# One queue of expert weights: issuing loads in reading order and varying the small expert's lag

## The chip, the cores and the metric

The kernel runs on 1 core of a Trainium2 chip. The metric is the device time of one execution in microseconds. The kernel before takes 1853.82 us (median of 3 runs, 1853.0 to 1855.28).

## What is computed

Two transformer-like blocks of two layers each on 256 tokens of width 1024. The change touches the last stage only, the mixture of experts of the second block: each token goes to the 2 best of 8 experts.

```python
logits = x @ router_w
top_v, top_i = lax.top_k(logits, TOP_K)              # TOP_K = 2 of N_EXPERTS = 8
gates = jax.nn.softmax(top_v, axis=-1)
combine = sum(one_hot(top_i, 8) * gates[..., None], axis=-2)
for e in range(8):                                   # D_FF_EXPERT = 3584
    y = y + combine[..., e:e+1] * ((silu(x @ w_gate[e]) * (x @ w_up[e])) @ w_down[e])
x = layer_norm(DEEPNORM_ALPHA * x + y, ln_ffn_g, ln_ffn_b)
```

The three weight matrices of the 8 experts are 336 pieces of 1 MB (128 partitions x 2048 floats). Each is read once from memory.

## The kernel before

**Blocks.** The experts are put in 8 places. The even places 0, 2, 4, 6 are "many" places with 128 token slots, the odd places 1, 3, 5, 7 are "few" places with 64 slots (32 in place 7), and the experts with fewer tokens go to the odd places. Each place is cut into 7 blocks (e, b) of 512 hidden columns. A block needs 6 pieces of weights: two of gate (`mgate`), two of up (`mup`), two of down (`mdown`).

**A many block** splits each piece: ScalarE rounds it to a high part (L437, into one of three `whi` buffers) and VectorE subtracts that for a low part (L438). TensorE multiplies the tokens' high and low parts with the high piece and the high part with the low piece: 8 + 4 matmuls for a piece. **A few block** uses the pieces as they are (`passing`), in plain fp32 matmuls that sit side by side in the array: gate and up of one half (hf) are read together, by `proj_few`.

**The order of blocks** is one list for everything. `at` gives many block i the place i in it and few block i the place i + `BEHIND`; the list is sorted by this. With `BEHIND` at 2.5 all along, three many blocks come first, then few and many alternate, and two few blocks are left at the end.

**Inside the loop over blocks** (L2021) block n projects its gate and up pieces, and between them `turn` transposes the hidden values of block n - 1; then `down` of block n - 1 follows. So for a few block n after a many block, TensorE reads: gate and up of half 0, gate and up of half 1, then the two down pieces of block n - 1. All these matmuls are chained in the order in which the program lists them (`self.line`, `kept`).

**The loads.** Every piece is one DMA of 1 MB on SyncE's queue (L385). `self.order` chains them in the order of the calls. A load goes to the next place in `self.ring`, a first-in first-out list of some 17 places of 1 MB (`raw`, `room`, `xlo`, `x`, and for the first 36 turns `my` and `oht`). It can be issued only once TensorE has read what was there, and the loads behind it wait too. A piece that is split keeps one place: its low part goes into the place left over from the piece before (`low`). For a few block after a many block the calls come in this order: the two down pieces of block n - 1 (L2044, kept in `WD`), gate and up of half 0, gate and up of half 1 (L1903). The loads of an expert other than that of place 0 use its number from a register, which SyncE reads (L2024) ahead of that expert's first load.

Of the kernel before, what the change touches and what calls it, by code (L numbers as in the profile page):

```python
# [33 lines left out]
RANKS = (None, 3, 0, 4, 1, 5, 2, 6)  # L34
SLOTS = (128, 64, 128, 64, 128, 64, 128, 32)

BEHIND = 2.5, 2.5

SPLITS = (("dsa_q", 256), ("dsa_k", 64), ("dsa_v", 64), ("idx_q", 256), ("idx_k", 32), ("idx_w", 8),
          ("fox_q", 384), ("fox_k", 384), ("fox_v", 384), ("fox_f", 6), ("nsa_q", 384), ("nsa_kc", 128),  # L40
# [243 lines left out]
class Net:  # L284
# [1410 lines left out]
    def _moe(self, x, out):  # L1695
# [9 lines left out]
        at = self.psum("t")  # L1705
        hold, kept = self.hold, []
        for tb in range(2):
            ts = slice(tb * 128, tb * 128 + 128)
            with self.ahead(5000):
# [22 lines left out]
                b = nc.vector.tensor_scalar(oh[:, tb, 0], self.c["iota"], slot[:, tb, 0:1], None, op0=ALU.is_equal)  # L1732

                for c in range(2):
# [5 lines left out]
                    i = self.split(xh[:, tb, cs], xl[:, tb, cs], p)  # L1740
                    if tb:
                        self.after(i, b)
                        b = i
# [19 lines left out]
        def back(oh, dt):  # L1763

            ohf = oh.bitcast(F32) if dt is F32R else oh
            oht = self.late.tile([128, NE, T], dt, name="oht", tag="oht")
            for e in range(0, NE, 2):
                p = self.psum()
                for i in range(2):
                    for tb in range(2):  # L1770
                        t = self.tr(p[:, i * 256 + tb * 128:i * 256 + tb * 128 + 128], ohf[:, tb, e + i], self.ident)
                        self.after(t, gm)
                i = nc.scalar.copy(oht[:, e:e + 2], p.rearrange("p (e t) -> p e t", e=2))
                self.after(i, gx)
            return oht
# [63 lines left out]
        i = nc.vector.tensor_copy(cnt, p)  # L1839
# [32 lines left out]
        def block_of(n, q, b, hf):  # L1872

            if q == 0:
                return d[n][0, b, hf]
            return d[n][bass.ds(expert[q], 1), b, hf].rearrange("e p n -> (e p) n")

        H, YD, PP, WD = {}, {}, {}, {}

        def proj(e, b, n, steps=iter(())):  # L1880

            es = slice(0, 128)
            p = self.psum()
            for hf in range(2):
                w = block_of(n, e, b, hf)
                h, lo = self.weights(w, hold=early.pop(0), pieces=range(4)) if early else self.weights(w)
                for i in range(4):
                    k, cs = hf * 4 + i, slice(i * 512, i * 512 + 512)
                    self.mm(p, gh[:, k, es], h[:, cs], start=k == 0, stop=False)
                    self.mm(p, gl[:, k, es], h[:, cs], start=False, stop=False)  # L1890
                if hf:
                    next(steps, None)
                for i in range(4):
                    k, cs = hf * 4 + i, slice(i * 512, i * 512 + 512)
                    self.mm(p, gh[:, k, es], lo[:, cs], start=False, stop=k == KC - 1)
                next(steps, None) if hf == 0 else None
            PP[e, b, n] = p

        def proj_few(e, b, hf):

            p = PP[e, b] = PP.pop((e, b)) if hf else self.psum()
            with self.ahead(3000):
                ws = [self.passing(block_of(n, e, b, hf)) for n in ("mgate", "mup")]  # L1903
            m = SLOTS[e]
            n = 8 * m
            for i in range(4):
                k = hf * 4 + i
                for r in range(0, 128, m):
                    w, c = ws[r // 64], r % 64 // m * n
                    self.mm(p[r:r + m, 0:n], FX[e][:, k, 0:m], w[:, i * 512 + c:i * 512 + c + n], start=k == 0,  # L1910
                            stop=k == KC - 1, tile_position=(0, r), skip_group_check=True)

        def act(e, b):
            sg = self.xp.tile([128, 512], F32, name="msg", tag="sq", bufs=2)
            if e % 2:
                n = 8 * SLOTS[e]
                nc.scalar.copy(sg[:, 0:n], PP.pop((e, b))[:, 0:n])
            else:
                self.after(nc.scalar.activation(sg, PP.pop((e, b, "mgate")), AF.Silu), self.parted[0])
                self.after(nc.vector.tensor_tensor(sg, sg, PP.pop((e, b, "mup")), op=ALU.mult), self.parted[1])  # L1920
            H[e, b] = sg

        def turn(e, b):
            sg = H.pop((e, b))
            pt = self.psum("t")
            m = SLOTS[e]
            for i in range(4 if m == 128 else m // 16):
                self.tr(pt[:, i * 128:i * 128 + 128], sg[:, i * 128:i * 128 + 128], self.ident)
            if e % 2:

                n, h = m // 16, 64 // m
                pv = pt[:, 0:n * 128].rearrange("p (i a m) -> p a i m", i=n, a=2)
                fs, fh = (sg[:, j * 256:j * 256 + n * 64].rearrange("p (i m) -> p i m", i=n) for j in range(2))
                nc.scalar.activation(fs, pv[:, 0], AF.Silu)
                nc.vector.tensor_tensor(fh, fs, pv[:, 1], op=ALU.mult)
                H[e, b] = [fh[:, f % n, f // n * m:f // n * m + m] for f in range(4)]
                return
            i = (7 * (e // 2) + b) % 2
            hh, hl = mh[:, i, 0], mh[:, i, 1]
            i = nc.scalar.copy(hh, pt), nc.vector.tensor_tensor(hl, pt, hh.bitcast(F32), op=ALU.subtract)  # L1940
            if (e, b) in WD:

                for a, p in zip(i, self.parted):
                    self.after(a, p)
            H[e, b] = hh, hl
# [67 lines left out]

        mh = None
        many, few = ([(e, b) for e in range(i, NE, 2) for b in range(7)] for i in range(2))
        at = {f: i + np.interp(i, (0, len(few) - 1), BEHIND) for i, f in enumerate(few)}
        at.update((m, i) for i, m in enumerate(many))
        blocks = sorted(at, key=at.get)
        first = blocks.index(few[0])
# [1 line left out]
        for n, (e, b) in enumerate(blocks):  # L2021
            if n == 2:
                for q in range(1, NE):
                    expert[q] = nc.values_load(idi[0:1, q:q + 1], engines=(mybir.EngineType.SP,), min_val=1, max_val=NE - 1)  # L2024
            if n == 9:

                mc = hw.tile([128, 1], F32, name="mc")
                over = hw.tile([128, 8], F32, name="over")

                nc.vector.memset(cap[:, 0:1], 128.0)  # L2030
                nc.vector.tensor_scalar(cap[:, 1:8], rank[:, 1:8], 2.5, 64.0, op0=ALU.is_lt, op1=ALU.mult)
                nc.vector.tensor_scalar(over[:, 1:8], rank[:, 1:8], 5.5, 32.0, op0=ALU.is_lt, op1=ALU.mult)
                nc.vector.tensor_tensor(cap[:, 1:8], cap[:, 1:8], over[:, 1:8], op=ALU.add)
                nc.vector.tensor_scalar(cap[:, 1:8], cap[:, 1:8], 32.0, None, op0=ALU.add)
                nc.vector.tensor_tensor(over, cnt, cap, op=ALU.subtract)
                nc.vector.tensor_reduce(mc, over, axis=AX.X, op=ALU.max)
                nc.vector.tensor_scalar(mc, mc, 0.0, None, op0=ALU.max)
                mci = hw.tile([128, 1], I32, name="mci")
                nc.vector.tensor_copy(mci, mc)
            if n == 7:  # L2040
                oht = back(oh, F32R)
            steps = iter(())
            if e % 2 and blocks[n - 1][0] % 2 == 0:
                WD[blocks[n - 1]] = [self.weights(block_of("mdown", *blocks[n - 1], hf)) for hf in range(2)]  # L2044
            if e % 2:
                proj_few(e, b, 0)
            else:
                proj(e, b, "mgate")
            if n == 1:
                mh = hw.tile([128, 2, 2, 512], F32R, name="mh", tag="mh")  # L2050
            if n:
                turn(*blocks[n - 1])
            if n + 1 == first:
                steps = gather(0, some=False)
            if e % 2:
                proj_few(e, b, 1)
            else:
                if b == 6 and e + 2 < NE:
                    steps = gather(e + 2)
                proj(e, b, "mup", steps)  # L2060
            act(e, b)
            if n < 2:

                i = by_place(qcomb, comb) if n else places(oh, qslot, range(1, NE), True)
                self.hold = self.hold[0], i, None
            if n:
                down(*blocks[n - 1], steps)
            for _ in steps:
                pass
            if n > 2 and blocks[n - 2][1] == 6:  # L2070
                scatter(blocks[n - 2][0])
            if n == len(blocks) - 5:
                gb = self.rows()
# [144 lines left out]
```

## Time and profile before

| | |
|---|---|
| time, median of 3 runs | 1853.82 us |
| the profiled execution | 1856.29 us |
| its span, first to last instruction | 1854.5 us |
| TensorE busy in the span | 1783.7 us (96%) |
| VectorE, ScalarE busy | 1073.1 us (58%), 867.3 us (47%) |
| mean granted TensorE clock | 0.982 |
| data moved | 497.71 MB, mean 268 GB/s |

The expert stage runs from about 1000 us to the end. Of its loads the first ten are issued before 975 us. A busy TensorE here is a TensorE that has a matmul under way; matmuls overlap, so the time of one and the distance between the starts of two are different numbers. The page's strip of DMA rates shows 394 to 421 GB/s from about the middle of that stage's first fifth to the end, and 102 to 338 GB/s before that.

### The profile page before, as it was taken

How to read it: one execution, taken by the hardware profiler on the slowest of the kernel's cores; microseconds unless marked ns; L12 is line 12 of the kernel's file. 1: busy time of each engine (PE TensorE's matmuls, PEld its weight loads, DVE VectorE, ACT ScalarE, POOL GpSimd, SP SyncE). 2: the span in 40 equal slices, each digit the busy share in tenths (PEclk: the TensorE clock that was granted, in tenths of full speed). 3: DMA queues.
4: the chain of work that ended last, by engine and by line, in shares of the span. 5: the costliest groups of instructions: out<-in, count | busy, mean ns of one | idle time of the engine just before them, and what ended most of it. 6: DMA issues, size and time to landing. Idle time of an engine off the chain costs nothing. (4 is left out here: it accounts for less than half of the span.)

```text
span 1854.5 us, 27561 instructions
## 1 busy us (share of the span) xinstructions
PE 1783.7 (96%) x11038; PEld 1351.6 (73%) x11038; DVE 1073.1 (58%) x1586; ACT 867.3 (47%) x1291; POOL 33.3 (2%) x78
## 2 busy tenths in 40 slices
PE   7999999999999999999999999999999999999984
PEld 5777788778896999888977766665656566665652
DVE  3765688757644754466437755565556565565543
ACT  3454375545553544345345545444535444444531
POOL 1000010000000000000010000000000000000000
PEclk9999999999999999989998999999999999999997
DMA  9654443234211555543028799999999999999996
GB/s 386 257 225 167 175 160 125 69 115 171 92 54 63 196 184 172 197 146 117 24 102 338 287 398 394 411 413 420 421 421 421 421 421 421 421 421 420 421 420 250
DMA packets 71175, 497.71 MB, mean 268 GB/s; under 512 B 8226, under 2 KB 9538, under 8 KB 11264
## 3 DMA queue, kind: packets, MB, share of 16 engines
q1 hardware_dynamic: 70752, 495.39, 67.8%
q8 instruction: 89, 1.46, 0.3%
q0 software_dynamic: 288, 0.48, 0.1%
q14 instruction: 46, 0.38, 0.1%
HBM read 493.81 MB, written 1.05 MB: 267 GB/s over the span
## 5 line engine op out<-in xcount | busy, mean ns | idle before, releaser
L438 DVE TENSOR_TENSOR raw<-raw,whi 128x2048 fp32r<-128x2048 f32 (+1 forms) x157 | 279.8, 1800 | 198.9 <-ACT whi L437 198.2
L437 ACT CAST whi<-raw 128x2048 fp32r<-128x2048 f32 (+1 forms) x198 | 306.6, 1570 | 160.7 <-PE mm L459 48.6
L413 PE MATMUL mm<-whi,g 128*128 128x512 f32 x896 | 227.3, 396 | 2.5 <-DVE y L2011 2.5
L413 PEld LDWEIGHTS mm<-whi,g 128*128 128x128 f32 x896 | 166.4, 189 | 38.9 <-issue 4.5
L437 ACT CAST whi<-room 128x2048 fp32r<-128x2048 f32 (+1 forms) x97 | 172.9, 1803 | 31.7 <-PE mm L413 13.5
L458 PE MATMUL mm<-xhi,whi 128*128 128x256 f32 x720 | 182.1, 288 | 0.7 <-ACT whi L437 0.7
L459 PE MATMUL mm<-xlo,whi 128*128 128x256 f32 x720 | 180.4, 286 | 0.0
L413 PE MATMUL mm<-room,fx 128*64 128x512 f32 (+1 forms) x632 | 152.1, 526 | 10.6 <-DMA room<-in_mup_dram 7.2
L458 PEld LDWEIGHTS mm<-xhi,whi 128*128 128x128 f32 x720 | 137.7, 191 | 8.1 <-issue 5.6
L459 PEld LDWEIGHTS mm<-xlo,whi 128*128 128x128 f32 x720 | 137.7, 191 | 1.5 <-issue 1.4
L438 DVE TENSOR_TENSOR room<-room,whi 128x2048 fp32r<-128x2048 f32 x47 | 107.6, 2289 | 31.7 <-ACT whi L437 29.7
L413 PE MATMUL s<-whi,mh 128*128 128x512 f32 x448 | 117.2, 404 | 0.0
L413 PEld LDWEIGHTS s<-whi,mh 128*128 128x128 f32 x448 | 82.6, 189 | 37.9 <-issue 19.9
L463 PE MATMUL mm<-xhi,raw 128*128 128x256 f32 x720 | 104.3, 285 | 0.0
L413 PE MATMUL mm<-raw,fx 128*64 128x512 f32 (+1 forms) x344 | 91.5, 508 | 6.5 <-DMA raw<-in_mup_dram 6.5
L1940 ACT CAST mh<-t 128x512 fp32r<-128x512 f32 x28 | 16.4, 585 | 169.5 <-PE t L416 169.4
L463 PEld LDWEIGHTS mm<-xhi,raw 128*128 128x128 f32 x720 | 93.6, 191 | 1.2 <-DVE cin L1219 0.9
L413 PEld LDWEIGHTS mm<-room,fx 128*64 128x64 f32 (+1 forms) x632 | 47.9, 129 | 57.4 <-issue 38.9
L438 DVE TENSOR_TENSOR raw<-room,whi 128x2048 fp32r<-128x2048 f32 x30 | 68.7, 2291 | 32.7 <-ACT whi L437 31.5
L438 DVE TENSOR_TENSOR room<-raw,whi 128x2048 fp32r<-128x2048 f32 x30 | 68.8, 2292 | 28.4 <-ACT whi L437 26.9
L1920 DVE TENSOR_TENSOR msg<-msg,mm 128x512 f32<-128x512 f32 x28 | 19.3, 688 | 100.5 <-PE mm L413 100.5
L413 PEld LDWEIGHTS mm<-raw,fx 128*64 128x64 f32 (+1 forms) x344 | 28.0, 125 | 47.6 <-issue 35.6
(590 smaller groups left out, 3264.3 us busy)
## 6 DMA issues: line engine op xcount, KB each, us to landing
room<-in_mup_dram SPq DMA_DIRECT2D x66, 1024.0 KB, 13.0
room<-in_mdown_dram SPq DMA_DIRECT2D x60, 1024.0 KB, 18.0
room<-in_mgate_dram SPq DMA_DIRECT2D x55, 1024.0 KB, 15.2
raw<-in_mdown_dram SPq DMA_DIRECT2D x41, 1024.0 KB, 17.1
raw<-in_mgate_dram SPq DMA_DIRECT2D x38, 1024.0 KB, 12.8
raw<-in_mup_dram SPq DMA_DIRECT2D x33, 1024.0 KB, 18.8
raw<-in_win_dram SPq DMA_DIRECT2D x29, 1024.0 KB, 6.4
raw<-in_din_dram SPq DMA_DIRECT2D x24, 1024.0 KB, 4.8
```

Source lines behind the costliest of these rows:

```text
L413: return self.kept(self.nc.tensor.matmul(*a, **k))
L437: a = nc.scalar.copy(h[:, v], r[:, v])
L438: b = nc.vector.tensor_tensor(lo[:, v], r[:, v], h[:, v].bitcast(F32), op=ALU.subtract)
L458: nc.tensor.matmul(out, w, xh[:, k], start=start and i == 0, stop=False)
L459: nc.tensor.matmul(out, w, xl[:, k], start=False, stop=False)
L463: nc.tensor.matmul(out, lo[:, off + i * 128:off + i * 128 + 128], xh[:, k], start=False, stop=stop and i == n - 1)
L1920: self.after(nc.vector.tensor_tensor(sg, sg, PP.pop((e, b, "mup")), op=ALU.mult), self.parted[1])
L1940: i = nc.scalar.copy(hh, pt), nc.vector.tensor_tensor(hl, pt, hh.bitcast(F32), op=ALU.subtract)
```

## The change

The program gives `BEHIND` as points for the interpolation: the lag is 2.5 at few block 0, 0.6 from few block 6 to few block 20, and 2.5 again at few block 27. In the sorted list, positions 6 to 53 change. The first pair of experts becomes (0,0) (0,1) (0,2) (1,0) (0,3) (1,1) (1,2) (0,4) (1,3) (0,5) (1,4) (1,5) (0,6) (1,6): two few blocks stand together twice, and the small expert ends with the large one. In the middle pairs many and few alternate, one few block earlier than before. The last pair ends with (6,5) (7,4) (6,6) (7,5) (7,6), where it was (7,3) (6,6) (7,4) (7,5) (7,6).

In the loop, the four loads of a few block (gate and up, both halves) are called ahead of the two down pieces of the many block before it, and kept in `GU` until `proj_few` uses them. The sums that are computed don't change.

```diff
-BEHIND = 2.5, 2.5
+BEHIND = (0, 6, 20, 27), (2.5, 0.6, 0.6, 2.5)
@@
-        H, YD, PP, WD = {}, {}, {}, {}
+        H, YD, PP, WD, GU = {}, {}, {}, {}, {}
@@ def proj_few(e, b, hf):
-            with self.ahead(3000):
-                ws = [self.passing(block_of(n, e, b, hf)) for n in ("mgate", "mup")]
+            ws = GU.pop((e, b, hf))
@@
-        at = {f: i + np.interp(i, (0, len(few) - 1), BEHIND) for i, f in enumerate(few)}
+        at = {f: i + np.interp(i, *BEHIND) for i, f in enumerate(few)}
@@ for n, (e, b) in enumerate(blocks):
             steps = iter(())
+            if e % 2:
+
+                with self.ahead(3000):
+                    for hf in range(2):
+                        GU[e, b, hf] = [self.passing(block_of(w, e, b, hf)) for w in ("mgate", "mup")]
             if e % 2 and blocks[n - 1][0] % 2 == 0:
                 WD[blocks[n - 1]] = [self.weights(block_of("mdown", *blocks[n - 1], hf)) for hf in range(2)]
```

## Rows read from the trace of the kernel before

**Rows 1.** Stretches: length; busy us (instructions) PE, PEld, DVE, ACT, POOL; clock; DMA share; GB/s
```profile
1200.00:1300.00 100.00, 98.98 (x451) 58.10 (x452) 57.97 (x40) 40.43 (x32) 0.00 (x0) 1.00 1.01 417
...
1600.00:1700.00 100.00, 99.29 (x492) 65.00 (x491) 62.46 (x43) 49.09 (x40) 0.00 (x0) 1.00 1.01 421
1700.00:1750.00 50.00, 42.39 (x306) 27.40 (x305) 24.74 (x15) 20.39 (x17) 0.00 (x0) 0.93 1.01 421
```

**Rows 2.** TensorE in order of time at (7,1): start us, us, count [idle before, releaser]
```profile
1706.16 1.92 PE L413 MATMUL mm<-raw,fx 128*32 128x256 f32 x28 [1.87 <-DMA raw<-in_mup_dram]
...
1711.13 3.59 PE L413 MATMUL mm<-room,fx 128*32 128x256 f32 x28 [1.86 <-DMA room<-in_mup_dram]
```

**Rows 3.** TensorE in order of time, the last reading of a piece
```profile
1837.03 1.59 PE L413 MATMUL o<-room,msg 128*32 128x256 f32 x16 [1.32 <-SPq L2086]
```

**Rows 4.** TensorE in order of time, from (1,0) through (0,3) to down of (0,3)
```profile
1054.16 1.09 PE L413 MATMUL s<-xlo,mh 128*128 128x512 f32 x4
...
1058.77 0.66 PE L416 MATMUL t<-lead,msg 128*128 128x128 f32 x4
1059.35 3.65 PE L413 MATMUL mm<-room,fx 128*64 128x512 f32 x16
1062.93 2.13 PE L413 MATMUL s<-whi,mh 128*128 128x512 f32 x8
1064.91 1.10 PE L413 MATMUL s<-oht,mh 128*128 128x512 f32 x4
...
1067.72 1.09 PE L413 MATMUL s<-x,mh 128*128 128x512 f32 x4
...
1070.51 1.07 PE L413 MATMUL mm<-raw,g 128*128 128x512 f32 x4
...
1079.16 1.07 PE L413 MATMUL mm<-room,g 128*128 128x512 f32 x4
1080.16 3.65 PE L413 MATMUL o<-raw,msg 128*64 128x512 f32 x16
...
1091.35 2.13 PE L413 MATMUL s<-whi,mh 128*128 128x512 f32 x8
```

**Rows 5.** The stretches after 1050 us that move least, same columns as Rows 1
```profile
1056.00:1066.00 10.00, 10.00 (x47) 4.72 (x44) 1.22 (x2) 3.53 (x4) 0.00 (x0) 1.00 0.34 135
1066.00:1076.00 10.00, 10.00 (x48) 8.16 (x47) 9.06 (x5) 6.31 (x6) 0.00 (x0) 1.00 0.90 340
...
1096.00:1106.00 10.00, 10.00 (x48) 8.18 (x47) 7.48 (x5) 6.50 (x5) 0.00 (x0) 1.00 0.99 398
...
1116.00:1126.00 10.00, 10.00 (x46) 5.20 (x43) 4.65 (x3) 5.40 (x6) 0.00 (x0) 1.00 0.81 330
1126.00:1136.00 10.00, 10.00 (x48) 8.22 (x47) 7.93 (x5) 6.33 (x6) 0.00 (x0) 1.00 0.98 380
...
1186.00:1196.00 10.00, 10.00 (x47) 8.21 (x46) 9.62 (x7) 7.16 (x8) 0.00 (x0) 1.00 0.96 373
...
1216.00:1226.00 10.00, 10.00 (x47) 8.18 (x47) 9.50 (x5) 6.36 (x6) 0.00 (x0) 1.00 0.98 382
```

**Rows 6.** SyncE's queue in order of time: start us, us, load
```profile
1055.28 0.34 SPq L385 DMA_DIRECT2D xlo<-in_mup_dram  x1
1066.04 0.33 SPq L385 DMA_DIRECT2D oht<-in_mgate_dram  x1
1068.85 0.33 SPq L385 DMA_DIRECT2D x<-in_mup_dram  x1
```

**Rows 7.** Loads issued from 1000 to 1020 us: count, KB each, us to landing
```profile
room<-in_mup_dram SPq DMA_DIRECT2D x1, 1024.0 KB, 4.8
```

**Rows 8.** Reads of the expert numbers: count: ns min/median/max, first and last start
```profile
L2024 SPq TENSOR_LOAD <-idi x7: 263/277/503, 1012.4 to 1651.4; - x7
```

**Rows 9.** Groups from 1000 us on: count, busy us, mean ns of one, idle before, releasers
```profile
L437 ACT CAST whi<-room 128x2048 fp32r<-128x2048 f32 x89 | 168.5, 1910 | 27.5 <-PE mm L413 13.5 <-PE s L413 9.3 <-DMA room<-in_mdown_dram 4.0
...
L438 DVE TENSOR_TENSOR room<-room,whi 128x2048 fp32r<-128x2048 f32 x47 | 107.6, 2289 | 31.7 <-ACT whi L437 29.7
```

## The prediction, made before the change was run

> **What bounds the kernel now.** I read the busy time by stretches first. From 1200 us on, the five 100 us stretches move 417 to 421 GB/s [rows 1], which I take for the ceiling of these loads: no stretch of that length goes at more. TensorE has no idle time to speak of in the same stretches, so the next question is which of the two is late at the end. TensorE in order of time answers it: from (7,1) on it waits for gate and up pieces, 1.87 and 1.86 us for one block [rows 2], and its last reading waits for its piece too and starts at 1837.03 [rows 3]. A pair of blocks agrees: TensorE goes from one many block's down to the next in 1091.35 - 1062.93 = 28.4 us [rows 4], while 12 pieces of 1.0486 MB at 421 GB/s take 12 x 2.49 = 29.9 us. Gathers and scatters fill the difference, until place 7, whose few blocks are shorter. So **the end is set by the loads**: 336 pieces, plus the time in which the DMA engines had nothing to do, plus a tail of 17.5 us from the last landing to the end of the span. Idle DMA time counts wherever it lies.
>
> The stretches of 10 us show where it lies [rows 5]. Against 421 GB/s the seven stretches there lose 6.8, 1.9, 0.5, 2.2, 1.0, 1.1 and 0.9 us, 14.4 us together; those between them and all later ones are within 4% of the ceiling. What is lost before 1056 I leave out: there many blocks alone hand out the places, and the change leaves that as it is. Their cause is in SyncE's queue: the load into xlo goes at 1055.28 and the next, into oht, at 1066.04 [rows 6]. TensorE's rows name the wait: oht holds the low part of a down piece, which is read from 1064.91 on [rows 4]. By then the four places of (1,0)'s gate and up had been free since 1058.8 and 1063.0 (the transposes and the down matmuls that follow their readings, [rows 4]), but those loads stand behind oht, because the down pieces were called first. TensorE reads gate and up first, the ring gives places back in the order of the calls, so each few block holds the queue once. As long as several loads are under way that costs nothing, which is why the hole is 6.8 us at the first few block and under 3 later.
>
> **The change, part by part.**
>
> *Loads in reading order.* Nothing is added: the same four loads of a few block are issued, ahead of two others. Each is 0.33 us on SyncE [rows 6], which otherwise waits. What it gives, by hand from the releases of [rows 4]: a load issued at 1055.2 (end of the reading of xlo) moves until about 1059; places come free at 1058.8 (two), 1063.0 (two), 1068.7 (the second down piece; oht is not used again, since its 36 turns are over), 1071.5, some 1074 and, because the place `my` has left the ring too, only at 1080.1 for the next. Of the 4.8 us that a load takes on an idle queue [rows 7] 2.49 are moving; I put 1.3 of the rest ahead of it and 1.0 behind (an estimate). So the engines are idle for about 1.1 us before the first of these and 3.6 us before the last, and without a hole between. So the 8.7 us of loss at 1056 to 1076 become 4.7, in part a little later. After 1080 places come free in the order of reading at 2.36 us each on average (28.4 / 12) against 2.49 us of moving, so the queue grows and the later holes go.
>
> *The lag of 0.6 from the first pair.* No work is added; blocks trade places. Two few blocks together give back 12 places in some 23 us (a few block takes 3.6 us for one half, 0.6 for transposes, 3.6 for the other half, 3.65 for its down, [rows 4]) where the loads need 29.9. That builds the queue just where the holes at 1096 to 1136 stand (0.5 + 2.2 + 1.0 us) and carries it past those at 1186 and 1216 (1.1 + 0.9). I let both parts together remove these 5.7 us whole. TensorE gets ahead of the loads by it and may wait earlier than at (7,1); while the DMA engines are busy, that wait costs nothing.
>
> *Sum for the last landing:* 14.4 - 4.7 = 9.7, say **10 us earlier**. Bounds: 14.4 if no hole is left; 4 if only the hole at 1056 goes (8.7 - 4.7) and the later ones stay.
>
> *The register ahead of the first few load.* That load used a place free at 1000 us for a down piece of place 0; now a load of place 1 is to go there and must wait for the first reading of an expert number, 1012.4 us [rows 8]. One load is 12 us later, at a time when TensorE hands out the places one by one. It is 2.5 us of moving, caught up in the gaps between those loads before 1056. I take 0; the bound is 2.5 us of loss. Later experts' readings are queued as before.
>
> *The down pieces are split last.* A down piece of a many block now lands after the gate and up of the few block. It needs 1.91 us on ScalarE and 2.29 us on VectorE [rows 9], and behind these two stand `turn`'s own split of the hidden values and the few block's copy. With a stock of landed pieces that is hidden. Where TensorE is level with the loads, in the last pair, it waits once per pair ahead of `down` instead of twice ahead of gate and up; the loads go on meanwhile, so 0 in the sum. What queues behind it on ScalarE and VectorE are the next block's splits, which land later anyway.
>
> *The tail.* (6,6) now stands third from the end, and its second down piece is followed by 8 loads, 19.9 us. Counted back from the last landing: split and `turn` about 5 us, down 5.7 us (1062.93 to 1068.65), the two halves of (7,6) 1.92 us each [rows 2] with transposes, down of (7,5) 2.1 us (half of it for one piece, [rows 3]), the scatter of place 6, eight matmuls like those of 2.13 us [rows 4], transposes and Silu of (7,6) 1.5 us: TensorE is ready for the last piece about 1 us after its landing where it now waits for it. If one of these bursts runs at the lower clock, that is 1.7 us more (3.59 against 1.92, [rows 2]; granted clock 0.93 in the stretch, [rows 1]). So 0 to 3 us; I take **2 us later**.
>
> Total: 10 - 2 = 8 us. The profiled execution took 1856.29 us for a span of 1854.5; it would become 1848.3. The runs' median is 2.5 us under that execution, so the forecast for the median is 1853.8 - 8 = **1845.8 us**.
>
> A rule that speaks against it: waits in one piece of 5 us and more take the place of short ones. [Rows 2] show what two short ones did: the burst behind the second took 3.59 us where 1.92 do at full speed. The Trainium skill, TensorE: Matmul & The Clock Gate, section "HAM oscillation — how this bites in real kernels", says that a wait for a load between bursts of matmuls lets the array fall back to the slow clock, so that each burst starts slow again. By that rule every pair of the last place would lose such a start; the trace agrees in kind.
>
> **The rivals.**
> 1. *Only half comes.* The later holes belong to the gathers, not to the order of calls, or the new hole of 3.6 us is larger: 4 to 6 us of landing, 2 of tail, about 1850. For it: the holes at 1186 and 1216 stand one block apart, as each few block's do, but they are so small that any wait of TensorE's would explain them.
> 2. *Nothing measurable.* The pieces come earlier but the places are handed out no faster, and idle DMA time moves to where the ring is full: within 3.7 us of 1853.8. That the order of issue doesn't follow the calls belongs here. Against it: after 1226 no stretch loses anything, so what is gained once isn't given back.
> 3. *Slower: TensorE at 1.2 GHz from (6,6) on.* The tail worked out above has some 17 us of TensorE work between that down piece and the last reading; at half speed it ends 17 us later, less the 10 us of earlier landing: 1861. It decides from the point where the tail grows by more than 13.7 us, that is if four fifths of the chain run at the low level. For it: the longer waits. Against it: of the two bursts after waits in [rows 2] one ran at full speed, and the waits in the tail are short.
>
> **How the numbers follow.** Forecast case, 5.5 to 13 us faster: 0.63. Rival 1: 0.19, of which some 0.13 is faster by over 0.2% (3.7 us, about what a measurement of this kernel can tell from none). Rival 2: 0.12. Rival 3: 0.06. Faster 0.76, same 0.17, slower 0.07. The range reaches from all holes filled with the tail's 2 us (1853.8 - 14.4 + 2 = 1841.4, put at 1841) to the bound of 4 us with a tail of 2 (1851.8).
>
> **What would show it.** Right: SyncE issues two loads near 1059 and two near 1063 where there was nothing until 1066; 1056 to 1066 moves 350 GB/s or more, and the stretches from 1086 on 417; the last reading starts 8 to 10 us earlier; in the last pair the waits stand ahead of the down of many blocks, 4 to 7 us each, and those ahead of gate and up are gone. Wrong: the rate at 1116 to 1136 stays at 330 to 380 (rival 1), a new stretch under 400 GB/s after 1226 (rival 2), or the last reading much later than the last landing (rival 3).

## The result, and the profile after

| | before | after |
|---|---|---|
| median, us (lowest to highest, 4 runs each) | 1854.55 (1853.0 to 1856.53) | 2048.26 (2046.31 to 2050.36) |
| span of the profiled execution, us | 1854.5 | 2045.4 |
| TensorE busy, us | 1783.7 | 1832.9 |
| mean granted clock of TensorE | 0.982 | 0.940 |

The changed kernel takes 1.1044 times as long (95% interval 1.1025 to 1.1063): 194 us slower, where 8 us faster was forecast.

The stretches say at once that the loads no longer set the end. Where the kernel before moved 417 and 421 GB/s with TensorE busy for 99% [rows 1], the changed one moves 310 to 338 in the six stretches from 1200 to 1800 us, and TensorE is busy for 79 to 86% at a clock of 0.86 to 0.92. Three of the six (columns: length; busy us of PE, PEld, DVE, ACT, POOL; clock; DMA share; GB/s):

```profile
1200.00:1300.00 100.00, 85.48 (x374) 54.23 (x371) 50.58 (x46) 37.74 (x34) 0.00 (x0) 0.90 0.86 332
1300.00:1400.00 100.00, 78.63 (x323) 45.73 (x322) 38.66 (x23) 32.59 (x25) 0.00 (x0) 0.87 0.89 337
1600.00:1700.00 100.00, 85.69 (x366) 52.73 (x367) 38.10 (x23) 30.83 (x24) 0.00 (x0) 0.91 0.89 338
```

The waits of TensorE from 1050 us on name what it waits for: us in total, times, longest.

```profile
PE s L413 <- ACT mh L1939: 110.2, 24, 4.8
PE s L413 <- DVE mh L1939: 54.1, 24, 2.5
PE mm L413 <- DVE y L2010: 1.4, 3, 0.5
```

It waits 24 times ahead of `s`, the down matmuls of a many block, for the split of the hidden values `mh` into a high and a low part, once on ScalarE and once on VectorE: 164.3 us. Before, all waits of TensorE from 1050 us on were 25 us, most of them for loads; the two largest groups:

```profile
PE mm L413 <- DMA room<-in_mup_dram: 7.2, 5, 1.9
PE mm L413 <- DMA raw<-in_mup_dram: 6.5, 4, 2.0
```

Now all are 167.1. That makes 142 us; 49.2 us more of busy time come on top (1832.9 - 1783.7); together 191, which is the difference of the spans (190.9). Of the busy time 48 us lie in one group of down matmuls (before, then after; count | busy us, mean ns of one | idle before):

```profile
L413 PE MATMUL s<-whi,mh 128*128 128x512 f32 x427 | 111.9, 404 | 0.0
L413 PE MATMUL s<-whi,mh 128*128 128x512 f32 x424 | 160.1, 525 | 164.4 <-ACT mh L1939 110.2 <-DVE mh L1939 54.1
```

Why `mh` is late stands in ScalarE's queue. First a pair of the kernel before, in order of time (start us, us, instruction, count [idle before, releaser]):

```profile
1341.44 0.59 ACT L1919 ACTIVATE msg<-mm 128x512 f32<-128x512 f32 x1
1341.92 1.90 ACT L437 CAST whi<-room 128x2048 fp32r<-128x2048 f32 x1
1343.71 1.91 ACT L437 CAST whi<-raw 128x2048 fp32r<-128x2048 f32 x1
1354.32 0.59 ACT L1940 CAST mh<-t 128x512 fp32r<-128x512 f32 x1 [8.69 <-PE t L416]
1357.91 0.59 ACT L1917 COPY msg<-mm 128x512 f32<-128x512 f32 x1 [3.01 <-PE mm L413]
```

Then the same place in the changed kernel, where these lines of the program have numbers lower by one:

```profile
1334.91 0.60 ACT L1918 ACTIVATE msg<-mm 128x512 f32<-128x512 f32 x1 [1.71 <-PE mm L413]
1335.40 0.38 ACT L1933 ACTIVATE msg<-t 128x256 f32<-128x256 f32 x1
1352.06 0.59 ACT L1916 COPY msg<-mm 128x512 f32<-128x512 f32 x1 [16.28 <-PE mm L413]
1352.54 1.90 ACT L437 CAST whi<-room 128x2048 fp32r<-128x2048 f32 x1
1354.34 1.90 ACT L437 CAST whi<-x 128x2048 fp32r<-128x2048 f32 x1
1356.14 0.59 ACT L1939 CAST mh<-t 128x512 fp32r<-128x512 f32 x1
```

Before, the two casts of the down pieces (L437) follow the many block's Silu (L1919) at once, and ScalarE then waits for the transposes with nothing left undone. After, the few block's copy out of PSUM, TensorE's result memory (L1916), stands ahead of them. It can only run when TensorE has finished both halves of `proj_few`, so ScalarE stands idle for 16.28 us, and the casts are stuck behind it although their pieces are there. These had been issued some 39 us before, and from 1323 to 1326 us nothing was moving, so by then they had landed:

```profile
1313.22 0.33 SPq L385 DMA_DIRECT2D room<-in_mdown_dram  x1
1313.79 0.33 SPq L385 DMA_DIRECT2D x<-in_mdown_dram  x1
```

The split of `mh` comes last of the four, because the program, before and after, holds it behind the casts of the down pieces (L1940 to L1943 of the changed kernel). TensorE, having finished `proj_few`, has the down next and nothing else:

```profile
1348.33 3.65 PE L413 MATMUL mm<-room,fx 128*64 128x512 f32 x16
...
1356.78 0.79 PE L413 MATMUL s<-whi,mh 128*128 128x512 f32 x1 [4.79 <-ACT mh L1939]
1359.81 3.35 PE L413 MATMUL s<-whi,mh 128*128 128x512 f32 x7 [2.23 <-DVE mh L1939]
1362.96 1.85 PE L413 MATMUL s<-xlo,mh 128*128 128x512 f32 x4
1364.65 2.03 PE L413 MATMUL s<-whi,mh 128*128 128x512 f32 x8
```

4.79 us is the copy, two casts and the split on ScalarE (0.59 + 1.90 + 1.90 + 0.59 = 5.0, less overlaps); 2.23 us more is VectorE, which makes the low part of the second down piece (2.29 us from 1356.86) before that of `mh` (0.68 us from 1359.07).

The burst behind the waits runs at half speed: 7 matmuls in 3.35 us, where 8 take 2.03 two lines on. The granted clock is 1.00 from 1344 to 1352 us and 0.50 from 1356 to 1363, that is 1.2 GHz in place of 2.4. Among the waits of the kernel before from 1050 us on there is none for `mh`.

What stays open is why the queue came out in this order. In both programs the casts are called ahead of the copy (L2048 and, in `act`, L2065 in the changed one); only the calls of the loads traded places. So it is the build of the kernel that put the copy first, and by what rule, no run here shows.

The loads themselves did what was forecast. SyncE issues two and two where it had nothing until 1066.04 before [rows 6], and 1056 to 1066 us moves 369 GB/s instead of 135 [rows 5]:

```profile
1057.12 0.34 SPq L385 DMA_DIRECT2D x<-in_mdown_dram  x1
1057.56 0.38 SPq L385 DMA_DIRECT2D raw<-in_mdown_dram  x1
1061.29 0.34 SPq L385 DMA_DIRECT2D raw<-in_mgate_dram  x1
1061.89 0.34 SPq L385 DMA_DIRECT2D room<-in_mup_dram  x1
```

### The profile page after: what moved, and what is told of

It is laid out like the page before. It is cut to its first block, busy times and chain, and to the rows that moved or that the text cites. A ratio compares the mean times of both kernels' runs of the same rounds, so it can differ in the third digit from the quotient of the medians.

```text
span 2045.4 us, 27702 instructions
## 1 busy us (share of the span) xinstructions
PE 1832.9 (90%) x11038; PEld 1387.0 (68%) x11038; DVE 1071.4 (52%) x1586; ACT 865.0 (42%) x1291; POOL 33.2 (2%) x78
## 5 line engine op out<-in xcount | busy, mean ns | idle before, releaser
L438 DVE TENSOR_TENSOR raw<-raw,whi 128x2048 fp32r<-128x2048 f32 (+1 forms) x170 | 309.6, 1837 | 256.6 <-ACT whi L437 256.2
L437 ACT CAST whi<-raw 128x2048 fp32r<-128x2048 f32 (+1 forms) x202 | 313.7, 1575 | 199.9 <-PE s L413 58.6
L413 PE MATMUL s<-whi,mh 128*128 128x512 f32 x448 | 166.2, 518 | 164.4 <-ACT mh L1939 110.2
L413 PEld LDWEIGHTS s<-whi,mh 128*128 128x128 f32 x448 | 110.2, 253 | 219.8 <-ACT mh L1939 129.0
L437 ACT CAST whi<-room 128x2048 fp32r<-128x2048 f32 (+1 forms) x93 | 165.4, 1797 | 88.6 <-PE s L413 73.0
L1916 ACT COPY msg<-mm 128x512 f32<-128x512 f32 (+1 forms) x28 | 14.9, 532 | 312.1 <-PE mm L413 312.1
L438 DVE TENSOR_TENSOR room<-raw,whi 128x2048 fp32r<-128x2048 f32 x27 | 61.9, 2291 | 89.2 <-ACT whi L437 89.0
L438 DVE TENSOR_TENSOR room<-room,whi 128x2048 fp32r<-128x2048 f32 x37 | 84.7, 2288 | 20.2 <-ACT whi L437 19.1
L413 PE MATMUL mm<-raw,fx 128*64 128x512 f32 (+1 forms) x280 | 85.5, 560 | 0.0
L438 DVE TENSOR_TENSOR xlo<-room,whi 128x2048 fp32r<-128x2048 f32 x11 | 25.2, 2292 | 83.5 <-ACT whi L437 83.5
L1919 DVE TENSOR_TENSOR msg<-msg,mm 128x512 f32<-128x512 f32 x28 | 19.2, 686 | 93.9 <-PE mm L413 93.9
```

The costliest lines, as they stand in the source:

```text
L413: return self.kept(self.nc.tensor.matmul(*a, **k))
L437: a = nc.scalar.copy(h[:, v], r[:, v])
L438: b = nc.vector.tensor_tensor(lo[:, v], r[:, v], h[:, v].bitcast(F32), op=ALU.subtract)
```

## The experiments

Theory A: the queue of ScalarE is the whole loss, and the order of the loads underneath gives time back. Rival B: the later issue of the down loads itself is the loss. Rival C: the lag is. Rival D: the clock is a cause, not an effect.

**The two parts apart.** The order of the loads alone, the lag left at 2.5:

```
-BEHIND = (0, 6, 20, 27), (2.5, 0.6, 0.6, 2.5)
+BEHIND = (0, 27), (2.5, 2.5)
```

> Only the order of the loads is changed; the small expert's lag stays at 2.5 blocks throughout. Theory A (ScalarE's queue: with the down loads issued behind the few block's four loads, the few block's copy out of PSUM stands ahead of the casts of the down pieces, and TensorE waits for them before each down): the waits of about 4.8 and 2.5 us in front of the downs of the many blocks are there as in the changed kernel, the loss is nearly all of the 194 us, some 2010 to 2060 us. Rival C (the lag: few blocks that come too early hold up the many ones): the loss is gone, 1843 to 1855 us.

Measured: 2055.01 us, 1.1081 times the kernel before (1.1061 to 1.1101). TensorE has 25 pairs of waits for `mh`, 111.7 and 55.6 us. The order of the loads brings the whole loss.

The lag alone, with the loads in the order of the kernel before:

```
-BEHIND = 2.5, 2.5
+BEHIND = (0, 6, 20, 27), (2.5, 0.6, 0.6, 2.5)
...
-        at = {f: i + np.interp(i, (0, len(few) - 1), BEHIND) for i, f in enumerate(few)}
+        at = {f: i + np.interp(i, *BEHIND) for i, f in enumerate(few)}
```

> Only the small expert's lag is changed (2.5, 0.6, 0.6, 2.5 over the blocks); the loads are issued in the order of the kernel before. Theory A: the casts of the down pieces stay ahead of the few block's copy on ScalarE, no loss; a small gain or none, 1846 to 1854 us. Rival C (the lag is the loss): 1950 to 2050 us.

Measured: 1854.15 us, ratio 0.9997 (0.9987 to 1.0007). Rival C falls. Alone, the lag gives no time that can be told from none. (The forecast put its 5.7 us on both parts together, which this run doesn't test.)

**The casts put back ahead.** One line in the changed kernel holds the few block's copy behind the last cast that was called, which is that of the down pieces:

```
-                nc.scalar.copy(sg[:, 0:n], PP.pop((e, b))[:, 0:n])
+                self.after(nc.scalar.copy(sg[:, 0:n], PP.pop((e, b))[:, 0:n]), self.parted[0])
```

> The changed kernel with one more line: the few block's copy out of PSUM is placed behind the two casts of the down pieces on ScalarE. The loads are issued as in the changed kernel. Theory A: the waits in front of the downs go and the time is the one that was forecast, 1842 to 1850 us. Rival B (the loss comes from the loads' order itself: the down pieces land or are split too late because their loads are issued later): it stays near 2040 us. Rival D (the clock is the cause and not an effect of the waits): it stays above 1900 us with a granted clock of 0.94 or less.

Measured: 1850.26 us, ratio 0.9978 (0.9967 to 0.9988); the profiled execution 1849.73. 198 us go with one edge, loads and lag untouched, and the mean clock is 0.980. Rivals B and D fall: the loads still come in the new order, and the clock comes back with the waits gone. The queue in the same place:

```profile
1335.65 0.60 ACT L1918 ACTIVATE msg<-mm 128x512 f32<-128x512 f32 x1 [1.78 <-PE mm L413]
1336.14 0.38 ACT L1933 ACTIVATE msg<-t 128x256 f32<-128x256 f32 x1
1340.70 1.91 ACT L437 CAST whi<-raw 128x2048 fp32r<-128x2048 f32 x1 [4.18 <-DMA raw<-in_mdown_dram]
1343.20 1.90 ACT L437 CAST whi<-room 128x2048 fp32r<-128x2048 f32 x1 [0.60 <-DMA room<-in_mdown_dram]
1349.18 0.59 ACT L1939 CAST mh<-t 128x512 fp32r<-128x512 f32 x1 [4.08 <-PE t L416]
1352.80 0.59 ACT L1916 COPY msg<-mm 128x512 f32<-128x512 f32 x1 [3.03 <-PE mm L413]
```

The casts now wait for their loads and are done 4 us before the transposes are. It is worth noticing that the stock of landed pieces is small in this run: the casts do wait for the DMA, 4.18 us here, but in time that ScalarE has.

The same line with the lag left at 2.5:

> Only the order of the loads is changed, the lag stays at 2.5, and the few block's copy is placed behind the two casts of the down pieces on ScalarE. Theory A: no waits in front of the downs, the order of the loads gives its own share, some 4 us: 1845 to 1852 us. Rival B: near the run with the order alone, 2010 to 2060 us.

Measured: 1849.22 us, ratio 0.998 (0.9969 to 0.9992). With the casts ahead, the order of the loads alone gives all that both parts give, as far as the intervals tell.

**The casts put behind in the kernel before.** The opposite: loads are called as before (down pieces first), lag as before, but the splits of the down pieces wait for the few block's copy, and that of the hidden values for them (`copied` holds the copy, `split` the two instructions that split `mh`):

```
-                WD[blocks[n - 1]] = [self.weights(block_of("mdown", *blocks[n - 1], hf)) for hf in range(2)]
+                with self.ahead(3000):
+                    landed = [self.raw_unit(block_of("mdown", *blocks[n - 1], hf)) for hf in range(2)]
...
+            if landed:
+                self.loaded, landed = landed, []
+                WD[blocks[n - 1]] = [self.weights(None, hold=(copied[0], self.hold[1])) for hf in range(2)]
+                for a, p in zip(split, self.parted):
+                    self.after(a, p)
```

> The loads' order and the lag are those of the kernel before; only the splits of the down pieces (ScalarE's casts and VectorE's subtractions) and, behind them, that of the many block's hidden values are queued behind the few block's copy out of PSUM. Theory A (the place of the casts on ScalarE is the whole loss): TensorE waits in front of each down of a many block as in the changed kernel, and the time is 1990 to 2060 us although no load was moved. Rival B (the loss needs the later issue of the down loads): near the kernel before, 1850 to 1880 us.

Measured: 2069.14 us, ratio 1.1149 (1.1133 to 1.1165). Its waits:

```profile
PE s L413 <- ACT mh L1941: 168.7, 26, 6.6
PE s L413 <- DVE mh L1941: 13.1, 26, 2.2
```

The down pieces were issued ahead of the few block's here (for instance two at 1043.04 and 1047.71, the gate piece after them at 1052.52), and the loss is there, somewhat larger. Two things did not stay as they were. A place is given to the ring where the split is called, so places come back in another order. And in the pair at 1338 us a third cast, one of the next many block's, stands between the copy and the split of `mh` (3 casts in 5.50 us, a wait of 6.59), so the 14 us above the order alone are no measure of theory A. With the runs before it this settles the cause from both sides: the casts behind the copy with the old order of loads, slow; the casts ahead of it with the new order, fast. What isn't tested is how much of each wait hangs on the program's holding `mh` behind the casts: a down needs its first cast in any case.

**Where the rest of the gain stays.** 8 us were forecast; with the casts ahead there are 4 to 5 (6.5 between the profiled executions). TensorE from 1640 us on in that run:

```profile
PE s L413 <- DVE mh L1939: 10.0, 5, 2.5
PE s L413 <- ACT mh L1939: 7.2, 4, 2.8
PE o L413 <- DVE msg L1934: 0.8, 1, 0.8
```

and its last waits of that kind, with the last reading of a piece (none of its waits from 1640 us on is for a load):

```profile
1811.31 0.49 PE L413 MATMUL s<-whi,mh 128*128 128x512 f32 x1 [2.04 <-ACT mh L1939]
1813.75 3.35 PE L413 MATMUL s<-whi,mh 128*128 128x512 f32 x7 [1.95 <-DVE mh L1939]
...
1830.65 1.05 PE L413 MATMUL o<-raw,msg 128*32 128x256 f32 x16
```

Theory E: in the last pair a down piece that lands just ahead of its reading still needs its casts, and the split of `mh` is held behind both casts; this wait sets the end. Rival F: loads and tail alone do. Three kernels, each from one with the casts ahead. In two, the last pair calls its down loads first again (with the new lag, then with 2.5 throughout):

```
+            late = e == NE - 1 and blocks[n - 1][0] % 2 == 0
+            if late:
+                WD[blocks[n - 1]] = [self.weights(block_of("mdown", *blocks[n - 1], hf)) for hf in range(2)]
             if e % 2:
...
-            if e % 2 and blocks[n - 1][0] % 2 == 0:
+            if e % 2 and blocks[n - 1][0] % 2 == 0 and not late:
```

> The changed kernel with the casts placed first, and in the last pair of experts (6 and 7) the down loads again ahead of the few block's four loads. Theory E (the missing 4 to 5 us of the gain: where loads are late, in the last pair, a down piece that lands just ahead of its reading still needs its two casts and the split of the hidden values, while a few block's piece needs none; in the reading order TensorE waits for that, 17.2 us in all from 1640 us on, the last time just ahead of the end): the waits in front of the downs go, and the time is 1843 to 1848 us, 2 to 5 us below the run with the casts first. Rival F (the loads alone set the end and the rest was lost in the tail or to the clock): 1849 to 1852 us, the same as that run.

> As the run with the order alone and the casts first (lag 2.5 throughout), and in the last pair the down loads ahead of the few block's four loads. Theory E: 1844 to 1848 us. Rival F: 1848 to 1851 us. Against the run before it in this set it shows what the shorter lag gives: by the lag_only run nothing, by the forecast 5 us.

Measured: 1849.84 us, ratio 0.9968 (0.9955 to 0.9981), and 1850.91 us, ratio 0.9974 (0.9965 to 0.9983). In the first the waits ahead of `s` are gone, but TensorE waits 12.4 us for gate and up pieces instead, and the last reading starts at 1830.46 against 1830.65. Both times lie where rival F has them: that wait is only moved.

In the third the loads stay in the new order, and in the last pair the split of `mh` is no longer held behind the casts:

```
-            if (e, b) in WD:
+            if (e, b) in WD and e < NE - 2:
```

> The changed kernel with the casts placed first, and in the last pair the split of the many block's hidden values no longer held behind the casts of the down pieces. Loads in the order of the changed kernel. Theory E: TensorE waits in front of a down for the first cast alone and no longer for two casts and the split, so some 2 to 4 us of each of the five waits ahead of the downs go, and the end comes 2 to 4 us earlier, 1846 to 1849 us. Rival F: 1849 to 1852 us.

Measured: 1848.06 us, ratio 0.9955 (0.9942 to 0.9968), a time that theory E named. Its trace doesn't bear the theory out: the waits ahead of `s` fall from 17.2 to 9.4 us, but new waits for loads (3.1 us of them put down to SyncE) take all 7.8 of it back. All waits from 1640 us on are 19.1 us against 19.2, and the last reading starts at 1830.88 against 1830.65. The gain over the run with the casts ahead is 0.23%, at the edge of what the intervals tell apart, so it was run again beside its twin with the old lag (the same line in the run with the order and the casts first):

> The same kernel as the run with the hidden values split first in the last pair, beside its twin with the old lag. If the gain of that run is real, 0.3 to 0.6% faster than before again, 1845 to 1850 us; if it was chance, at 0.2% like the run with the casts first alone.

> Order of the loads as in the changed kernel, casts placed first, hidden values split first in the last pair, but the lag of the small expert stays at 2.5 throughout. If the shorter lag gives what the forecast put on it (5.7 us), this run is 3 to 6 us slower than its twin; if the order of the loads alone takes the later holes away, as the rates of the earlier runs say, the two agree within 2 us.

Measured: 1846.77 us, ratio 0.9955 (0.9941 to 0.9969) again, and for the twin 1850.15, ratio 0.9972 (0.9962 to 0.9982). The changed kernel with the casts ahead and, in the last pair, the hidden values split first is **0.45% faster than the kernel before**, the best of all these. Its distance to the twin, 3.4 us, is the one sign in the times of a gain from the lag; the intervals overlap, so how much of it is real stays open. Where the gain over the run with the casts ahead comes from is open too, since the waits didn't become less: theory E isn't shown.

## Why the prediction was wrong, point by point

*What bounds the kernel, the holes* (right). With the casts ahead, loads at 1059.16, 1059.60, 1063.33 and 1063.92 stand where the forecast had two near 1059 and two near 1063, and the stretches read:

```profile
1056.00:1066.00 10.00, 10.00 (x48) 4.57 (x45) 1.62 (x3) 3.21 (x4) 0.00 (x0) 1.00 0.98 364
1066.00:1076.00 10.00, 10.00 (x47) 8.19 (x46) 9.40 (x5) 6.77 (x6) 0.00 (x0) 1.00 0.93 359
1076.00:1086.00 10.00, 10.00 (x46) 5.30 (x46) 5.18 (x3) 3.11 (x2) 0.00 (x0) 1.00 0.84 317
1086.00:1096.00 10.00, 10.00 (x47) 5.31 (x44) 0.69 (x1) 1.18 (x2) 0.00 (x0) 1.00 0.99 372
1096.00:1106.00 10.00, 10.00 (x49) 3.90 (x49) 0.42 (x1) 1.04 (x3) 0.00 (x0) 1.00 1.00 420
```

Against 421 GB/s these lose 1.4, 1.5, 2.5 and 1.2 us, 6.5 together, where [rows 5] lose 14.4 (14.8 with 1086 to 1096, which moved 404). So 8.3 us of holes go; 10 were forecast. What remains lies at 1056 to 1096, most of it from 1076 on, and is 1.8 us larger than its estimate of 4.7.

*Lag of 0.6* (right for both parts together, but little of it is the lag's). The 5.7 us of later holes were put on both together, and with both and the casts ahead they are gone. With the order and the casts alone, lag 2.5, 1116 to 1126 moves 421 and 1126 to 1136 moves 419, against 330 and 380 [rows 5]: the order of the loads takes these two away by itself. It leaves 1.3 us at 1176 to 1196 and 1216 to 1226 (401, 407 and 401 GB/s), which the lag takes. Summed over the stretches of 10 us from 1056 to 1800 us that move under 408 GB/s, the holes are 14.9 us before, 11.8 with the lag alone, 7.8 with the order and the casts, 6.5 with all three; in the times the lag's share isn't seen.

*The register ahead of the first few load* (right, 0). The first few load goes at 1010.13, and at 1012.15 with the casts ahead; between 1000 and 1050 us the stretches of 10 us lose 14.3 us against 421 GB/s in that run, 14.5 before.

***The down pieces are split last*: this step failed.** It saw that the two splits, `turn`'s split and the few block's copy share ScalarE, said "with a stock of landed pieces that is hidden", and entered 0. It asked when the pieces land, and took the place of the casts in ScalarE's queue as given: ahead of the copy, as before. The stock was there: the two pieces above had landed some 29 us before the first of their casts ran. But the queue came out of the build in another order, though the program calls the casts ahead of the copy as before. What stands ahead of the casts now is an instruction that waits for TensorE, and TensorE's next work waits for the casts. In place of 0 the term measures 142 us of waiting and 49 us of slower matmuls. A warning was in the trace: the copy of the few block waits for TensorE in every pair (3.01 us ahead of L1917 above, 90.8 us in 28; 312.1 us in 28 after the change), so anything that comes to stand behind it waits for the end of `proj_few`. That something would, no row of the kernel before could show. The step did name who queues *behind* the casts; it did not ask what they might come to queue behind.

*The tail* (right in kind). In the last pair the waits do stand ahead of the down of many blocks, 4.0 us in the one shown above and 4.7 at the longest (4 to 7 forecast), and three bursts behind them run at the lower clock (3.35 us for 7 matmuls). From 1820 us on, in slices of 0.5 us, the loads of the kernel before and of the run with both parts and the casts ahead come to their end like this:

```profile
GB/s 459 377 442 393 426 410 410 426 393 410 442 393 426 426 410 459 410 393 442 377 360 279 262 311 279 279 246 213 246 115 33 66 16 0 0 0 0 0 0 0
...
GB/s 393 442 426 344 295 279 279 311 262 229 246 246 213 197 164 66 33 33 16 0 0 33 0 0 0 0 16 0 33 0 33 0 0 0 0 16 33 0 0 0
```

The rate falls under 100 GB/s at 1835 before and at 1827.5 after: 7.5 us earlier. The last reading starts 6.4 us earlier (1837.03 in [rows 3], now 1830.65) and no longer waits for its piece; so the tail grew by 1.1 us, 2 were forecast. These are single executions; the spans are 6.5 us apart, the medians 4.8.

*The rule that speaks against it* (right, and undersized). The forecast applied it to the last pair alone. With 24 pairs that wait up to 4.8 and 2.5 us, the downs start slow: the 424 matmuls `s<-whi,mh` from 1050 us on take 525 ns each (404 before), and 1352 to 1375 us has a granted clock of 0.78, that is part of the time at 1.2 GHz in place of 2.4. The Trainium skill, TensorE: Matmul & The Clock Gate, section "HAM oscillation — how this bites in real kernels", describes this falling back between bursts, there behind waits for loads. The trace agrees, here behind waits for ScalarE and VectorE, with 49 us more of busy TensorE.

*The rivals.* Rivals 1 and 2 don't describe the result. Rival 3 had the right sign for another reason: the clock, in the tail, by loads. The clock is the smaller part of the loss here, and it follows the waits: with the casts ahead it is back at 0.980. Had the casts stayed ahead, the result would have been the 1850 us of that run, inside the range, with 4 to 5 us gained for the 8 forecast.

## What to carry to other kernels

Moving the call of a load can change what stands ahead of the casts that hang on it, in queues that the change doesn't mention: here casts and copy kept their order in the program and lost it in ScalarE's queue. Before costing a moved step at nothing, ask for each engine what could come to stand directly ahead of it, and whether that instruction waits for the engine that waits for the step; if so, fix the order by hand, as one edge did here. A gain of some microseconds from better transfers is lost many times over by one such place in every block.

## What the runs showed of the hardware

A wait can be paid twice on TensorE: 142 us more waiting came with 49 us more of busy time, because 7 matmuls behind a pair of waits of 4.8 and 2.2 us take 3.35 us (0.48 each, at a granted clock of 0.50) instead of 0.25 to 0.27 each. Shorter pairs do it too: in the run with the casts ahead, 2.04 and 1.95 us with one matmul between them are followed by 3.35 us again, while a single wait of 1.47 us is not:

```profile
1786.41 1.91 PE L413 MATMUL s<-whi,mh 128*128 128x512 f32 x7 [1.47 <-DVE mh L1939]
```

And transfers that were the limit before are not a limit that stays: with a DMA share of 1.01 they moved 421 GB/s from 1600 to 1700 us [rows 1], and 338 at a share of 0.89 in the changed kernel, because places come free only once TensorE has read them, and TensorE was waiting.
